# A decoder trunk with its memory values formed token by token, its first output tiles loaded early, and its delta-rule inverses set together by fours

## The chip, the cores and the metric

The kernel runs on one core of a Trainium2 chip. The metric is device time in microseconds of one execution; less is better. The core's engines are TensorE (PE, with its weight loads as PEld), VectorE (DVE), ScalarE (ACT), GpSimd (POOL) and SyncE (SP); all transfers go through the core's 16 DMA engines, issued by SP, by ACT or, in the changed kernel, twice by POOL.

## What is computed

Two layers on a sequence of 1024 tokens of width 1024, with 256 memory tokens for the cross attention. The first layer mixes tokens by an S5 state space model with a gated linear unit (GLU) behind it, the second by a chunked gated delta rule (chunks of 64). Cut to what matters here:

```python
for i in range(2):
    h = rmsnorm(x, norm_w[i]); mem_h = rmsnorm(mem, mem_norm_w[i])
    proj = h @ (s5_w_in if i == 0 else gdn_w_in)
    # layer 0: y = gelu(s5(u) + d*u); y = y * sigmoid(y @ w_glu + b_glu); y_mix = y * silu(gate)
    # layer 1: y_mix = rmsnorm(gated_delta_chunked(...)) * silu(gate)
    k, v = split(mem_h @ w_mem_kv[i]);  y_x = softmax(q k / sqrt(128)) v * silu(gate_x)
    x = x + concat([y_mix, y_x]) @ w_out[i]
return rmsnorm(x, final_norm_w)
# gated delta: per chunk and head  t_mat = (I + strict_lower(k_beta k^T * decay))^-1
```

## The kernel before

Every large product is made of three matmuls of fp32r halves, high by high, low by high and high by low (`mm3`, L48): names that end in h or `hi` are the high half, l or `lo` the low one. A weight tile is loaded as `wraw` (512 KB), its high half `whi` is a cast on ACT (L86), its low half `wlo` a subtraction on DVE (L73), or half of it on DVE and half on POOL. Activations lie feature by token, so that the weights are the stationary operand of 128x512 products.

*Front.* `memory_inputs` loads the memory `memT` (four loads of 256 KB). `memory(0)` weights it by the norm's weight (`mh`, `ml`), and makes eight column tiles of 128 features by 256 tokens with 24 matmuls each: four of keys, four of values. Each tile is multiplied by the row `mrow` of the memory's norms (`kvt`, DVE). A tile of values is then transposed on PE (`ps_a<-ident,kvt`, L51), copied by ACT (`kvu`, L278), and stored. The tokens' x is loaded, weighted (`hh`, `hl`) and projected for two S5 inputs; then `memory(1)` does the second layer's eight tiles. After that, S5 groups and the remaining input tiles of layer 0 run interleaved, with DVE and ACT about as full as PE.

*GLU and output projection.* Twelve GLU tiles (L739 on) read `y`, make 72 matmuls of 512 columns each, and store their result `ye` in DRAM as `yT[ct]`. The attention of layer 0 stores `yT[12]` to `yT[15]` beside it. When all pools of the GLU are closed (`gs.close()`), the loop over two halves of the tokens loads 16 tiles `yr` of `yT` (128x512), splits each to `oh` (ACT) and `ol` (DVE), and projects them to eight column tiles of `w_out`, in the order 12, 13, 14, 15, 0, 1, ..., 11.

*Gated delta units.* `g_units` (L1104 on) writes a table of steps by hand. One step of projection (6 matmuls of 512 columns) stands between two entries. For each of 16 units (chunk, half of the heads) it sets: `prepare` (decays E, from DRAM rows, DVE and the exponentials on ACT, L996), `scores`, `lower` (six transposes `ps_a<-ident,Eb`, which need DVE's `Eb`), `load` (blocks `N`, `T` of a partial inverse, from `Dn`, `Dt` in DRAM), and four stages of `inverse`, each of small products on PE and copies on ACT (`Y1`, L1074; `N`, L1084 to L1098; `Y2`, L1093). PE keeps this order.

*Tail.* `last_column` makes the last output tile in two blocks of 256 tokens, and `out_scale` scales eight tiles by the final norm: most on DVE, those listed in `beside` by ACT and POOL.

Of the kernel before, what the change touches and what calls it, by code (L numbers as in the profile page):

```python
# [22 lines left out]
L = 1024  # L23
# [30 lines left out]
class Kern:  # L54
# [62 lines left out]
    def weight(self, src, cols=128, nk=8):  # L117
        ring = next(self.rings)
        raw = ring.tile([128, nk, cols], F32, name="wraw", tag="wraw")
        hi = ring.tile([128, nk, cols], F32R, name="whi", tag="whi")  # L120
        lo = ring.tile([128, nk, cols], F32R, name="wlo", tag="wlo")
        with self.tc.high_priority(offset=self.ahead):
            self.wq.dma_start(out=raw, in_=src)
            self.split(raw, hi, lo, self.wlo_eng)
        return hi, lo
# [115 lines left out]
    def memory_inputs(self, wp):  # L241
        mt = self.memT = self.once(wp, (128, 8, 256), "memT")
        with self.tc.high_priority(offset=5000):
            self.dma(self.mnw, self.A["mnw"])

            self.act.copy(self.once(wp, (128, 1), "table"), self.ones[:, 0:1])
            for k in range(0, 8, 2):
                self.dma(mt[:, k:k + 2], self.A["memT"][k:k + 2].rearrange("k p t -> p k t"))

    def memory_norm(self, wp):  # L250
# [7 lines left out]
        mcol = self.rstd_cols(wp, acc, 1024, "mn")  # L258
        self.mrow = self.once(wp, (128, 256), "mrow")
        self.rows_to(self.mrow, self.on_partitions(wp, mcol, "mn"))  # L260

    def memory(self, layer, wp):
        mt = self.memT
        hh, hl = self.tl(wp, (128, 8, 256), "mh", F32R), self.tl(wp, (128, 8, 256), "ml", F32R)
        for k in range(8):
            self.weighted(mt[:, k], self.mnw[:, layer, k:k + 1], hh[:, k], hl[:, k])
        if layer == 0:
            self.memory_norm(wp)
        for ct in range(8):
            ps, = self.project([self.A["w_kv"][layer, ct]], (hh, hl), n=256)  # L270
            t = self.tl(wp, (128, 256), "kvt", bufs=2)
            self.tt(t, ps, self.mrow, MUL)
            if ct >= 4:
                pt = self.pa.tile([128, 512], F32, name="ps_a", tag="ps_a")
                for b in range(2):
                    self.pe.transpose(pt[:, 128 * b:128 * b + 128], t[:, 128 * b:128 * b + 128], self.ident)
                t = self.tl(wp, (128, 256), "kvu", bufs=2)
                self.act.copy(t, pt[:, 0:256])  # L278
            self.dma(self.kvd[layer][ct], t)


# [397 lines left out]
    def layer1(self):  # L679
        tc, A = self.tc, self.A  # L680
        P = partial(tc.tile_pool, reuse_waits="tile")
        with P(name="h1", bufs=1) as hp:
            h = self.hidden(hp)
            with P(name="s5p", bufs=1, side="right") as sp:
                with P(name="s5tmp", bufs=1, side="right") as tmp, P(name="mem", bufs=1, side="right") as mp:
                    self.memory_inputs(mp)
                    self.dma(self.nw, A["nw"])
                    self.rings = cycle([self.ring, self.ring, mp])
                    with P(name="ld1", bufs=1, side="right") as wp:
# [6 lines left out]
                        self.wlo_eng, self.wq = "both", self.nc.sync  # L696
                        with self.tc.high_priority(offset=self.ahead):
                            self.memory(0, mp)
                        self.wlo_eng, self.wq = self.v, self.nc.scalar
                        for k in range(KD):  # L700
# [17 lines left out]
                with P(name="s5w", bufs=2, side="right") as wp:  # L718
# [10 lines left out]
                    self.pe.on = False  # L729
            gs = ExitStack()  # L730
            ya = gs.enter_context(P(name="ya", bufs=1, side="right"))
            wp = gs.enter_context(P(name="glu", bufs=2, side="right"))
            ap = gs.enter_context(P(name="at1", bufs=1, side="right"))
            y = []
# [20 lines left out]
        for ct in range(12):  # L755
            w = A["w_glu"][ct]
            ps = self.project([w[:, 0:6], w[:, 6:12]], y)
            e, g = self.tl(wp, (128, L), "ye"), self.tl(wp, (128, L), "ge")
            self.dma(g, self.gate[ct])
            self.tt(e, y[ct][0].bitcast(F32), y[ct][1].bitcast(F32), ADD, self.pool)  # L760
            self.tt(e, e, g, MUL, self.pool)
            for j, p in enumerate(ps):
                s = slice(512 * j, 512 * j + 512)
                sg = self.tl(wp, (128, 512), "sig")
                self.act.activation(sg, p, AF.Sigmoid, bias=self.b_glu[:, ct:ct + 1])
                self.tt(e[:, s], e[:, s], sg, MUL)
            self.dma(self.yT[ct], e)
            for i in range(2):
                next(attend, None)
# [10 lines left out]
        with P(name="yo", bufs=1, side="right") as yp, P(name="x1", bufs=1, side="right") as xp:  # L780
# [3 lines left out]
            for half in range(2):  # L784
                hs, ts_ = slice(512 * half, 512 * half + 512), slice(4 * half, 4 * half + 4)
                y = self.half_tiles(yp, 512, lambda i: 2 if i < 4 else 1)
                for i, k in enumerate([12, 13, 14, 15] + list(range(12))):
                    t = self.tl(xp, (128, 512), "yr", bufs=8)
                    self.dma(t, self.yT[k, :, hs])
                    self.split(t, y[i][0], y[i][1])  # L790
                for ct in range(KD):
# [14 lines left out]
                    else:  # L806
                        sq = self.tl(xp, (128, 512), "sq", bufs=2)
# [3 lines left out]
            self.rows_to(h[2], self.on_partitions(xp, col, "n2"))  # L811
        return st2, h

    def half_tiles(self, yp, n, bufs):
        return [[self.tl(yp, (128, n), f"o{c}{i}", F32R, bufs(i)) for c in "hl"] for i in range(16)]

# [284 lines left out]
    def g_units(self, h, wp, gp):  # L1101
# [32 lines left out]
        for u in range(16):  # L1134
            s = 7 * u
            put(s - 9, prepare, u)
            put(s, scores, u)
            put(s + 5, lower, u)

            s = 80 + 6 * u if u < 4 else 124 + 4 * (u - 4) if u < 10 else 148 + 4 * (u - 10)  # L1140
            put(s - 5, load, u)
            for j in range(4):
                put(s + 3 * j, inverse, u)
        for i, s, n in ((0, 41, 26), (1, 83, 26), (2, 111, 22)):
# [205 lines left out]
    def last_column(self, wp, pieces, y, add, xo, acc):  # L1350
# [229 lines left out]
```

## Time and profile before

| what | value |
|---|---|
| median of 3 runs | 1933.11 us (1930.89 to 1936.47) |
| the profiled execution's own time | 1939.14 us |
| its span on the core | 1937.4 us |
| mean granted TensorE clock | 0.984 |
| PE busy | 1865.1 us, 96% |
| DVE, ACT, POOL busy | 1284.0, 958.1, 95.8 us |
| share of PE in the chain that ended last | 80% |

A row of the windows gives busy time (and instruction counts) of each engine in a stretch, then the clock that TensorE was granted (1.00 is full speed), the share of the DMA engines, and GB/s. A row of the timeline gives the start, the busy time, the engine, line, operation, tiles, and in brackets the idle time just before and what ended it. Times are microseconds from the start of the span.

### The profile page before, as it was taken

To read this page: it belongs to the slowest core of one execution; us is meant where nothing else is said; L and a number is where in the kernel's file an instruction comes from. 1 tells how busy PE (TensorE), PEld (TensorE's weight loads), DVE (VectorE), ACT (ScalarE), POOL (GpSimd) and SP (SyncE) were. 2 spreads that over 40 slices of the span, in tenths; PEclk is the share of its full clock that TensorE was granted. 3 is DMA by queue.
4 is the path that set the end of the run, shared out by engine and by line. 5 is a ranking of instruction groups with operands and counts; after the bars stand their busy time and mean duration, and the time that the engine had idled before them with its cause. 6 is when DMAs were issued, how large, how long until landed. Compare 5 with 4: busy or idle time off the path is not lost.

```text
span 1937.4 us, 28738 instructions
## 1 busy us (share of the span) xinstructions
PE 1865.1 (96%) x10390; PEld 1533.5 (79%) x10390; DVE 1284.0 (66%) x2508; ACT 958.1 (49%) x2043; POOL 95.8 (5%) x65
## 2 busy tenths in 40 slices
PE   6899999999989998999999999999999999899997
PEld 6788888788878887788778878877777888688886
DVE  7988898896565412564455555988743776789744
ACT  5345688786455421543343456665343653544421
POOL 3000000000201221000000000000000000000000
PEclk9999999999999999999999999999999999999999
DMA  7445655655854353654312467676445764876752
GB/s 229 151 136 136 165 170 157 168 155 146 254 167 133 116 173 102 210 164 141 120 56 97 132 199 235 218 224 198 132 117 197 226 202 146 265 231 197 201 161 87
DMA packets 258942, 325.17 MB, mean 168 GB/s; under 512 B 80753, under 2 KB 182705, under 8 KB 258801
## 3 DMA queue, kind: packets, MB, share of 16 engines
q1 hardware_dynamic: 233456, 238.40, 39.9%
q10 hardware_dynamic: 25344, 84.95, 14.7%
q8 instruction: 82, 1.34, 0.3%
q14 instruction: 60, 0.48, 0.1%
HBM read 213.20 MB, written 93.95 MB: 159 GB/s over the span
## 4 chain that ended last, share of the span: by engine, by line
PE 80%; DVE 7%; DMA 6%; ACT 4%; issue 2%; SPq 1%; DVEq 0%; ACTq 0%
PE pp L48 64%; PE ps_a L48 13%; PE ps_a L51 3%; DMA zr<-oTd 1%; SPq L70 1%; DVE wlo L73 1%; DMA yr<-gy 1%; ACT whi L86 0%; DVE pr L77 0%; DMA E<-Grow 0%; DVE ol L73 0%; ACT pr L330 0%; DMA XM<-Dm 0%; DMA R<-E 0%; DMA wraw<-in_s_w_in_dram 0%
## 5 line engine op out<-in xcount | busy, mean ns | idle before, releaser
L48 PE MATMUL pp<-hh,whi 128*128 128x512 f32 x1216 | 496.0, 408 | 0.0
L48 PE MATMUL pp<-hl,whi 128*128 128x512 f32 x1216 | 478.9, 394 | 2.8 <-DVE hl L82 2.8
L48 PE MATMUL pp<-hh,wlo 128*128 128x512 f32 x1216 | 478.0, 393 | 0.0
L86 ACT CAST whi<-wraw 128x1024 fp32r<-128x1024 f32 (+1 forms) x180 | 183.7, 1022 | 370.6 <-PE pp L48 347.0
L73 DVE TENSOR_TENSOR wlo<-wraw,whi 128x1024 fp32r<-128x1024 f32 (+2 forms) x180 | 212.9, 1183 | 94.4 <-ACT whi L86 93.2
L48 PEld LDWEIGHTS pp<-hh,whi 128*128 128x128 f32 x1216 | 229.7, 189 | 50.8 <-issue 5.3
L48 PEld LDWEIGHTS pp<-hh,wlo 128*128 128x128 f32 x1216 | 229.3, 189 | 48.9
L48 PEld LDWEIGHTS pp<-hl,whi 128*128 128x128 f32 x1216 | 230.1, 189 | 46.0 <-DVE hl L82 3.8
L48 PE MATMUL pp<-oh,whi 128*128 128x512 f32 (+1 forms) x528 | 207.8, 394 | 5.7 <-ACT oh L86 5.5
L48 PE MATMUL pp<-oh,wlo 128*128 128x512 f32 (+1 forms) x528 | 210.0, 398 | 0.1
L48 PE MATMUL pp<-ol,whi 128*128 128x512 f32 (+1 forms) x528 | 208.4, 395 | 1.3 <-DVE ol L73 1.3
L48 PEld LDWEIGHTS pp<-oh,whi 128*128 128x128 f32 x528 | 100.9, 191 | 29.0 <-ACT oh L86 7.7
L48 PEld LDWEIGHTS pp<-ol,whi 128*128 128x128 f32 x528 | 100.6, 191 | 25.8 <-DVE ol L73 3.5
L48 PEld LDWEIGHTS pp<-oh,wlo 128*128 128x128 f32 x528 | 101.0, 191 | 21.2 <-DVE wlo L73 0.8
L48 PE MATMUL pp<-yl,whi 128*128 128x512 f32 x288 | 114.2, 396 | 0.4 <-DVE yl L73 0.4
L48 PE MATMUL pp<-yh,wlo 128*128 128x512 f32 x288 | 114.2, 396 | 0.0
L48 PE MATMUL pp<-yh,whi 128*128 128x512 f32 x288 | 113.7, 395 | 0.0
L73 DVE TENSOR_TENSOR pj<-pp,hr 128x512 f32<-128x512 f32 x104 | 69.0, 686 | 54.8 <-PE pp L48 54.8
L73 DVE TENSOR_TENSOR cx<-pp,hr 128x512 f32<-128x512 f32 x48 | 32.5, 689 | 93.6 <-PE pp L48 93.6
L82 DVE SCALAR_TENSOR_TENSOR pj<-cx,conv_w,pj 128x1024 f32<-128x1024 f32 x72 | 92.4, 1283 | 1.4
L48 PEld LDWEIGHTS pp<-yl,whi 128*128 128x128 f32 x288 | 54.4, 189 | 12.4 <-DVE yl L73 0.8
L48 PEld LDWEIGHTS pp<-yh,wlo 128*128 128x128 f32 x288 | 54.4, 189 | 11.9
(363 smaller groups left out, 3109.2 us busy)
## 6 DMA issues: line engine op xcount, KB each, us to landing
wraw<-in_w_out_dram ACTq DMA_DIRECT2D x64, 512.0 KB, 4.1
wraw<-in_g_w_in_dram ACTq DMA_DIRECT2D x44, 512.0 KB, 3.9
wraw<-in_s_w_in_dram ACTq DMA_DIRECT2D x32, 512.0 KB, 4.0
R<-E SPq DMA_DIRECT2D x48, 256.0 KB, 3.9
gate<-pj SPq DMA_DIRECT2D x24, 512.0 KB, 4.4
qkv<-pj SPq DMA_DIRECT2D x24, 512.0 KB, 2.6
kq<-qkv SPq DMA_DIRECT2D x60, 192.0 KB, 4.3
wraw<-in_w_glu_dram ACTq DMA_DIRECT2D x24, 384.0 KB, 3.5
```

The lines of the kernel that those rows point to most:

```text
L48: return self.pin(self.eng.matmul(*a, **kw))
L51: return self.pin(self.eng.transpose(*a, **kw))
L70: self.nc.sync.dma_start(out=out, in_=in_)
L73: (eng or self.v).tensor_tensor(out=out, in0=a, in1=b, op=op)
L82: self.v.scalar_tensor_tensor(out=out, in0=a, scalar=s, in1=b, op0=op0, op1=op1)
L86: self.act.copy(hi, src)
```

## The change

Four places, the diff below cut to its core.

1. *Front.* The two weight tiles of the values of column tiles 4 and 5 are loaded first, in pieces, between the pieces of the memory. Values are made token by feature: the memory's blocks are the stationary operand, and two column tiles of weights are the moving one, so nothing is transposed; ACT scales them by the column `mcol` of the norms into one buffer `kvu`. Values come before keys, and PE is held to the program's order. The sum for the memory's norm is by additions instead of two reductions. `memory(1)` is built in the same way.
2. *GLU to output projection.* `out_inputs` loads and splits `yT[12..15]` and `yT[0]` for the first half of the tokens while the GLU still runs, into tiles of the attention's pool, which stays open. The next ten loads of the first half go straight to tiles of the `yo` pool that are free by then. The last two stores of `yT` are issued by POOL.
3. *Gated delta units.* `lower` comes at step s+7 instead of s+5. The inverses start at steps 84, 88, 92, 96 and then from 120 in fours, with four steps between stages instead of three; the first four have their blocks loaded eight steps ahead.
4. *Tail.* Block 0 of the last scaling has six of its eight tiles on ACT and POOL instead of four.

```diff
+            for q, step in ((0, 2), (1, 4)):
...
+                for k in range(4 * q, 4 * q + 4, step):
+                    raw, hi, lo = (t.rearrange("p (c k) n -> p c k n", c=2)[:, :, k % 4:k % 4 + step] for t in w)
+                    self.dma(raw, self.A["w_kv"][0, 4:6, :, k:k + step].rearrange("c p k n -> p c k n"))
+                    for j in range(k, k + step, 2):
+                        self.dma(mt[:, j:j + 2], self.A["memT"][j:j + 2].rearrange("k p t -> p k t"))
+                    self.split(raw, hi, lo)
...
-            self.v.tensor_reduce(out=part, in_=sq.rearrange("p k t -> p t k"), axis=AX, op=ADD)
+            self.tt(sq[:, 0:2], sq[:, 0:2], sq[:, 2:4], ADD)
+            self.tt(part, sq[:, 0], sq[:, 1], ADD)
...
+                        self.mm3(ps[b].rearrange("p (c n) -> p c n", c=2), (hh[:, k, s], hl[:, k, s]),
+                                 [t[:, j] for t in rows], k == 0, k == 7)
...
-            if ct >= 4:
-                pt = self.pa.tile([128, 512], F32, name="ps_a", tag="ps_a")
-                for b in range(2):
-                    self.pe.transpose(pt[:, 128 * b:128 * b + 128], t[:, 128 * b:128 * b + 128], self.ident)
...
+            t = self.tl(wp, (128, 2, 2, 128), "kvu", bufs=1)
+            for b in range(2):
+                self.act.activation(t[:, :, b], ps[b].rearrange("p (c n) -> p c n", c=2), AF.Copy,
+                                    scale=self.mcol[:, b:b + 1])
...
+            if ct == (0 if layer else 2):
+                for i, ps in enumerate(pairs):
+                    values(i, ps)
...
+            if ct == 10:
+                early = self.out_inputs(ap, wp)
...
-            self.dma(self.yT[ct], e)
+            (self.nc.sync if ct < 10 else self.pool).dma_start(out=self.yT[ct], in_=e)
...
+                    if half == 0 and n < 10:
+                        t = self.tl(yp, (128, 512), f"o{'hl'[n % 2]}{n // 2}")
...
+        for i, y in enumerate(tiles):
+            if i % 2 == 0:
+                raw = self.tl(wp, (128, L), "yr")
+            t = raw[:, 512 * (i % 2):512 * (i % 2) + 512]
+            self.dma(t, self.yT[(12, 13, 14, 15, 0)[i], :, 0:512])
+            self.split(t, *y)
...
-            put(s + 5, lower, u)
+            put(s + 7, lower, u)
...
+            s = 84 + 4 * u if u < 4 else 120 + 4 * (u - 4)
...
-        self.out_scale(wp, xo, rb, 1, blocks[0], (1, 3, 5, 7))
+        self.out_scale(wp, xo, rb, 1, blocks[0], (1, 3, 4, 5, 6, 7))
```

Three places where instructions move, all on ACT, whose products PE waits for. The first is the middle of `memory(0)`. Before, ACT's queue there holds the copies of the transposed values (`kvu`) among the casts of weights (`whi`) and the work on x (`hh`, `sq`):

```order
L86 CAST whi<-wraw 128x1024
L278 COPY kvu<-ps_a 128x256 x2
L179 ACTIVATE sq<-x 128x1024
L237 ACTIVATE hh_167<-x,nw_158 128x1024
L86 CAST whi<-wraw 128x1024
L278 COPY kvu<-ps_a 128x256
L86 CAST whi<-wraw 128x1024
```

Now the values come from the accumulators, and the second pair stands behind two tiles of x:

```order
L86 CAST whi<-wraw 128x1024
L313 ACTIVATE kvu<-ps_a,mcol_381 128x2x128 x2
L86 CAST whi<-wraw 128x1024
L242 ACTIVATE hh_167<-x,nw_158 128x1024
L184 ACTIVATE sq<-x 128x1024
L242 ACTIVATE hh_167<-x,nw_158 128x1024
L184 ACTIVATE sq<-x 128x1024
L313 ACTIVATE kvu<-pp,mcol_381 128x2x128 x2
```

The buffer `kvu` is one now, so the row `kvu<-pp` also waits until the two stores of the row `kvu<-ps_a` have landed; the third key tile on PE takes an accumulator that this row frees.

The second place is the end of the GLU. Before, the casts of the output projection's inputs (`oh`) all follow the last sigmoid (`sig`) and the cast of a small weight (`abw`):

```order
L765 ACTIVATE sig<-pp,b_glu_161 128x512
L86 CAST whi<-wraw 128x1024
L765 ACTIVATE sig<-pp,b_glu_161 128x512
L123 DMA wraw<-in_w_out_dram 128x1024
L86 CAST abw_7023<-abw_7022 128x8x24
L86 CAST oh_7035<-yr 128x512
```

Now five such casts, to tiles of the attention (`qh`, `ph`, `pr`, `q`), stand some forty rows ahead, beside the eleventh GLU tile; these are four of them:

```order
L86 CAST qh<-yr 128x512
L393 CAST ph<-ps_a 128x512 x2
L86 CAST ph<-yr 128x512
L86 CAST whi<-wraw 128x768
L86 CAST ph<-yr 128x512
L128 DMA wraw<-in_w_glu_dram 128x768
L86 CAST pr<-yr 128x512
```

What is left behind the last sigmoid are the casts from the sixth tile on.

The third place is the first group of inverses. Before, one cast of decays (`E`) stands right ahead of two copies of different inverses (`Y`):

```order
L1008 ACTIVATE kq<-ps_a,rk_9686 128x256 x3
L929 ACTIVATE pj<-pj 128x1024
L996 ACT_TABLE_LOAD
L996 ACTIVATE E<-E,gnG_8497 128x128 x6
L1093 COPY Y_11433<-ps_a 64x384
L1074 COPY Y_11448<-ps_a 32x192 x2
L1098 ACTIVATE N_9710<-ps_a 64x6x64
```

Now:

```order
L1171 ACTIVATE N_9675<-ps_a 32x6x32
L1172 ACTIVATE T_132_9679<-ps_a 32x6x32
L1082 ACT_TABLE_LOAD
L1082 ACTIVATE E<-E,gnG_8462 128x128 x6
L1160 COPY Y_11403<-ps_a 32x192 x2
L1184 ACTIVATE N_9674<-ps_a 64x6x64
L1179 COPY Y_11476<-ps_a 64x384
```

The copies of different inverses stand closer together, and a row of decays still stands ahead of them.

More of the change, by code (lines that the diff above doesn't have):

```diff
@@ L246, in memory_inputs, with memory_sum @@
             self.act.copy(self.once(wp, (128, 1), "table"), self.ones[:, 0:1])
-            for k in range(0, 8, 2):
-                self.dma(mt[:, k:k + 2], self.A["memT"][k:k + 2].rearrange("k p t -> p k t"))
-    def memory_norm(self, wp):
+            self.first = []
+            for q, step in ((0, 2), (1, 4)):
+                w = [self.ring.tile([128, 8, 128], dt, name=n, tag=n)
+                     for n, dt in (("wraw", F32), ("whi", F32R), ("wlo", F32R))]
+                self.first.append(w[1:])
+                for k in range(4 * q, 4 * q + 4, step):
[4 more added lines that the diff above has]
+                    self.split(raw, hi, lo)
+    def memory_sum(self, wp):
         acc = self.once(wp, (128, 256), "macc")
@@ L266, in memory @@
             self.weighted(mt[:, k], self.mnw[:, layer, k:k + 1], hh[:, k], hl[:, k])
+        pairs = []
+        for i in range(2):
+            pool, nm = ((self.pa, "ps_a"), (self.pp, "pp"))[i]
+            ps = [pool.tile([128, 256], F32, name=nm, tag=nm) for _ in range(2)]
+            for q in range(2):
+                w = self.first[q] if layer == i == 0 else self.value_weight(layer, i, q)
+                rows = [t.rearrange("p (c k) n -> p k c n", c=2) for t in w]
+                for j in range(4):
+                    k = 4 * q + j
+                    for b in range(2):
+                        s = slice(128 * b, 128 * b + 128)
+                        self.mm3(ps[b].rearrange("p (c n) -> p c n", c=2), (hh[:, k, s], hl[:, k, s]),
+                                 [t[:, j] for t in rows], k == 0, k == 7)
+            pairs.append(ps)
@@ new lines, in values @@
+        def values(i, ps):
+            t = self.tl(wp, (128, 2, 2, 128), "kvu", bufs=1)
+            for b in range(2):
+                self.act.activation(t[:, :, b], ps[b].rearrange("p (c n) -> p c n", c=2), AF.Copy,
+                                    scale=self.mcol[:, b:b + 1])
+            for c in range(2):
+                self.dma(self.kvd[layer][4 + 2 * i + c], t[:, c].rearrange("p b d -> p (b d)"))
+        todo = []
+        for ct in range(4):
+            if ct == (0 if layer else 2):
+                for i, ps in enumerate(pairs):
+                    values(i, ps)
+            ps, = self.project([self.A["w_kv"][layer, ct]], (hh, hl), n=256)
+            todo.append((ct, ps))
+            if layer == 0 and ct == 2:
+                self.mrow = self.once(wp, (128, 256), "mrow")
+                self.rows_to(self.mrow, self.on_partitions(wp, self.mcol, "mn"))
+            if layer or ct >= 2:
+                for one in todo:
+                    key(*one)
+                todo = []
@@ L811, in layer1, with out_inputs, half_tiles @@
             self.rows_to(h[2], self.on_partitions(xp, col, "n2"))
+        as1.close()
         return st2, h
-    def half_tiles(self, yp, n, bufs):
-        return [[self.tl(yp, (128, n), f"o{c}{i}", F32R, bufs(i)) for c in "hl"] for i in range(16)]
+    def out_inputs(self, ap, wp):
+        two = [self.tl(ap, (128, 2, 512), nm, F32R) for nm in ("ph", "pl")]
+        tiles = [[self.tl(ap, (128, 512), nm, F32R) for nm in ("qh", "ql")]]
+        tiles += [[t[:, b] for t in two] for b in range(2)]
+        tiles.append([self.tl(ap, (128, 512), nm, F32R) for nm in ("q", "sg")])
+        pr = self.tl(ap, (128, 2, 512), "pr", F32R)
+        tiles.append([pr[:, i] for i in range(2)])
+        for i, y in enumerate(tiles):
[4 more added lines that the diff above has]
+            self.split(t, *y)
+        return tiles
+    def half_tiles(self, yp, n, bufs, down=False):
+        order = range(15, -1, -1) if down else range(16)
+        y = {i: [self.tl(yp, (128, n), f"o{c}{i}", F32R, bufs(i)) for c in "hl"] for i in order}
+        return [y[i] for i in range(16)]
     def s5_input(self, i, h, wp):
```

48 lines of the change are left out of this document (30 added, 18 removed).

## Prediction

> **What bounds the kernel now.** I read the page's busy shares first (PE 96%), then the windows by stage, the waits of PE, and the timeline of PE at the longest of these. Of the windows, these stretches matter:
>
> ```profile
> 105.00:340.00 235.00, 235.00 (x1302) 195.06 (x1301) 200.79 (x382) 157.15 (x315) 0.00 (x0) 1.00 0.55 153
> 760.00:785.00 25.00, 19.29 (x66) 14.22 (x65) 13.23 (x20) 11.77 (x20) 0.00 (x0) 0.80 0.52 161
> 1140.00:1160.00 20.00, 16.54 (x70) 13.48 (x70) 10.77 (x14) 15.58 (x34) 0.00 (x0) 0.91 0.75 246
> 1285.00:1320.00 35.00, 30.53 (x276) 24.45 (x275) 29.86 (x59) 20.55 (x48) 0.00 (x0) 0.95 0.75 220
> ```
>
> PE is full where nothing is said of it, as from 105 to 340. So what can be won is idle time of PE, and with it stretches where the granted clock falls (0.80, 0.91, 0.95 here). The waits of PE name the places that this change touches:
>
> ```profile
> PE pp L48 <- ACT oh L86: 5.5, 2, 3.6
> PE ps_a L51 <- DVE kvt L73: 5.2, 2, 2.8
> PE ps_a L51 <- DVE Eb L73: 4.1, 3, 3.5
> PE ps_a L48 <- DVE fndg L79: 4.0, 1, 4.0
> PE ps_a L48 <- ACT Y L1093: 3.1, 1, 3.1
> PE pp L48 <- DVE hl L82: 2.8, 2, 2.0
> ```
>
> An idle stretch costs more than itself. At the start of the output projection (timeline of PE):
>
> ```profile
> 766.73 0.39 PE L48 MATMUL pp<-yh,wlo 128*128 128x512 f32 x1
> 770.74 0.50 PE L48 MATMUL pp<-oh,whi 128*128 128x512 f32 x1 [3.63 <-ACT oh L86]
> ...
> 775.83 0.80 PE L48 MATMUL pp<-oh,whi 128*128 128x512 f32 x1 [1.86 <-ACT oh L86]
> ...
> 780.14 0.63 PE L48 MATMUL pp<-oh,whi 128*128 128x512 f32 x1
> 780.56 0.63 PE L48 MATMUL pp<-ol,whi 128*128 128x512 f32 x1
> ...
> 781.40 0.39 PE L48 MATMUL pp<-oh,whi 128*128 128x512 f32 x1
> 781.63 0.39 PE L48 MATMUL pp<-ol,whi 128*128 128x512 f32 x1
> ```
>
> From start to start a matmul of 512 columns takes 0.42 us at 780 and 0.23 at 781.4: after the idle time PE ran at half speed. The Trainium skill ("TensorE: Matmul & The Clock Gate", Part 1: The HAM clock gate) has the same two rates and a window of about 3.4 us after which full speed returns; the trace agrees with the rates, and here the slow stretch lasts about 10 us, because a second idle time falls into it.
>
> **The change part by part.**
>
> *Output projection.* 18 matmuls of 512 columns stand between 766.73 + 0.23 and 781.40, that is 14.4 us for 18 x 0.23 = 4.1 us of work: 10.3 us are lost, 5.7 of them idle. Now 5 of 16 inputs lie ready; their 15 matmuls (15 x 0.23 = 3.4 us) run at once. Their loads and casts lie beside the last two GLU tiles, where ACT has room (11.77 of 25 us busy in the window above, most of it behind the GLU). The sixth input's cast still comes behind the last sigmoid, about when the idle time now ends (3.6 us behind the GLU), so those 3.4 us cover it or nearly, and the casts behind it, half of 1.05 us each, keep ahead of three matmuls (0.69). What is late next is the last input, `yT[11]`: POOL issues its store, and its load and cast must follow. No row shows a transfer from POOL. The page's lines for SP and ACT (section 6) bound it:
>
> ```profile
> gate<-pj SPq DMA_DIRECT2D x24, 512.0 KB, 4.4
> qkv<-pj SPq DMA_DIRECT2D x24, 512.0 KB, 2.6
> ```
>
> With an estimated 3 us for the last sigmoid and product of `ye`, 2.6 to 4.4 for the store, 4 for the load and 1.3 for cast and split, `yT[11]` is ready 11 to 13 us behind the GLU. By the order of PE its first matmul is the 51st behind the GLU, 50 x 0.23 = 11.4 us. I take a wait of 1.5 us: gain 8.5 us, with 4 (POOL's store 5 us late, and a slow clock behind it) and 10 as ends. The Trainium skill ("DMA: Bandwidth & Descriptors", Anatomy of one DMA) gives about 2.0 us plus bytes by 436 GB/s for a transfer issued by POOL, 3.2 us for this store by its fit; no run here shows it, and the sum by it would be the same.
>
> *Front.* These rows carry it (PE's timeline, the last three being the first matmul on x, of `memory(1)`, and behind it; and the first uses on ACT):
>
> ```profile
> 10.98 0.58 PE L48 MATMUL pp<-mh,whi 128*128 128x256 f32 x1 [10.98 <-ACT whi L86]
> 39.52 0.44 PE L51 MATMUL ps_a<-ident,kvt 128*128 128x128 f32 x2 [2.81 <-DVE kvt L73]
> 47.22 0.39 PE L48 MATMUL pp<-hh,whi 128*128 128x512 f32 x1
> 77.09 0.28 PE L48 MATMUL pp<-mh,whi 128*128 128x256 f32 x1
> 77.21 0.28 PE L48 MATMUL pp<-ml,whi 128*128 128x256 f32 x1
> 104.71 0.39 PE L48 MATMUL pp<-hh,whi 128*128 128x512 f32 x1
> 4.91 1.71 ACT L237 ACTIVATE mh<-memT,mnw 128x256 fp32r<-128x256 f32 x4 [2.62 <-DMA memT<-in_memT_dram]
> ```
>
> A matmul of 256 columns takes 0.12 us (77.09 to 77.21), so 192 of them take 23 us, once per layer, before and after alike. The first memory piece is on hand at 4.91 us; the first weight piece (256 KB, half the cast of 1.05 us) goes just ahead of it, so PE can start at about 6.2 instead of 10.98: 4.8 us. The eight transposes of layer 0 go (8 x 0.11 = 0.9), and the wait of 2.81 with a slow stretch behind it (1.7: half of one 3.4 us stretch, as at 1150 below). The waits on `hl` (2.8) go if the x loads come no later. Against this stands a new wait: the third key tile needs the accumulators of the second pair of values, and the row that frees them stands on ACT behind two tiles of x, about 1.15 + 1.05 us each, and behind the landing of two stores. The values' scale is known by about 25 us, the stores are issued by 28 and land near 31.5, and the row ends near 33.5, when PE wants it at 28 to 29: 5 us, and up to 3 us of slow clock. I take 6.5. Sum to 77.09: 4.8 + 0.9 + 2.8 + 1.7 + 2.8 - 6.5 = 6.5 us. In `memory(1)` the other `kvt` wait (5.2 - 2.81 = 2.4), a slow stretch (1.7) and eight transposes (0.9) go; the stores of its values have all of the second pair's time to land: 5 us. DVE loses two reductions and eight of 16 `kvt` products, and ACT eight copies, so neither is later. Together 11.5 us at 104.7.
>
> Does that pass through the S5 stage, where DVE is busy 201 of 235 us? The waits of DVE in that stretch:
>
> ```profile
> DVE pj L73 <- PE pp L48: 12.7, 5, 5.6
> DVE vs L73 <- ACT vw L642: 8.0, 6, 3.3
> DVE wbt L73 <- DMA bcs<-in_s_bc_dram: 5.1, 1, 5.1
> ```
>
> DVE waits for PE for 12.7 us in all, so PE leads there and DVE has about as much slack as PE wins. I take 2 us as lost on the way: 9.5 us for the front, with ends of 2 (all slack already used, and the new wait at 10) and 14.
>
> The half-speed start is in the sum as it was. By the same section of the Trainium skill, about 3.4 us of steady work would end it; before, it lasted from 10.98 until about 23.6 with two idle stretches in it, so the sum by that rule would be up to 4 us lower if the pieces come in time. That no row shows.
>
> *Gated delta units.* These rows, of PE and ACT:
>
> ```profile
> 1150.27 1.54 PE L51 MATMUL ps_a<-ident,Eb 128*128 128x128 f32 x6 [3.46 <-DVE Eb L73]
> 1311.94 1.05 PE L48 MATMUL ps_a<-Y,T 64*64 64x64 f32 x13 [3.06 <-ACT Y L1093]
> 1309.67 1.86 ACT L996 ACTIVATE E<-E,gnG 128x128 f32<-128x128 f32 x6
> 1311.44 0.45 ACT L1093 COPY Y<-ps_a 64x384 f32<-64x384 f32 x1
> ```
>
> `lower` two steps later puts 12 matmuls (2.7 us) into the wait of 3.46; the rest of `Eb` waits (0.6) goes, and with 0.7 us of idle time left there is no slow stretch (the clock of 0.91 over 20 us is 1.7 us): 5 us. For the inverses, the wait of 3.06 and its slow stretch (0.95 over 35 us, 1.7) come from a copy queued behind decays that were late. The order shows such a row of decays still ahead of the copies, but a stage now has four steps (5.5 us) instead of three. On the other side the first four start four steps apart instead of six, so that more copies stand behind each of the decays of steps 82, 89 and 96; and the other twelve start at 120 instead of 124, with their loads three steps (4 us) earlier, while their blocks are made in the same steps as before: a load that has to wait for them is a new wait of PE. I take a gain of 1 us, between +5 (the wait goes) and -5 (one more like it): 6 us for the stage, ends 0 and 10.
>
> *Tail.* On DVE the last norm's chain holds two scalings fewer:
>
> ```profile
> 1926.29 0.16 DVE L77 TENSOR_SCALAR fzh<-fzv 128x2 f32<-128x2 f32 x1
> 1926.35 0.47 DVE L82 SCALAR_TENSOR_TENSOR xo<-xo,fnw,ps_a 128x256 f32<-128x256 f32 x1
> 1926.74 0.31 DVE L79 TENSOR_SCALAR fze<-fze 128x2 int32<-128x2 int32 x1
> ```
>
> Each takes 0.4 us of a chain that PE waits 4.0 us for: 0.8 us. POOL has six products instead of four and is done before the last block needs it. Ends 0 and 1.2.
>
> **The sum.** 8.5 + 9.5 + 6 + 0.8 = 24.8 us off the profiled execution's 1939.14, to 1914.3. That execution lies 6 us above the median of 1933.11; off the median it is 1908.3, and I say 1909.
>
> **The rivals.** *The front's gain is used up in the S5 stage or by the new `kvu` wait.* For it: DVE is at 85% of that stage, and PE has waits on DVE and ACT behind it already. Against it: the 12.7 us above. Without the front's 9.5 us the time is 1918. *The last input comes late.* The stores by POOL are the one price that no row shows; with 5 us more and a slow stretch of the kind at 771 to 781, 7 us of the 8.5 are gone: 1916. *The change does less than it says*: the early inputs' loads wait for the last stores of `yT` or for space, and the front's pieces come as late as now. Then 5 us of the units and the tail are left: 1927. *Slower:* the store of `yT[11]` by POOL is slow in itself, since its price is the one that no row bounds from above. The first column can't end without it, and PE runs out of other work once it has the second column's ready inputs too: at 40 us instead of 4.4 the time is 1909 + 36 = 1945, and from 28 us on the change loses. Against it: POOL is idle there (0.00 in the window 760 to 785), and nothing else of POOL stands behind the store.
>
> **How the numbers follow.** The forecast, within its own ends, has 0.62; the front lost 0.12; the late input 0.1; less than it says 0.07; slower by POOL's store 0.05; 0.04 for gains beyond the upper ends. The ends added give 2 + 4 + 0 + 0 = 6 us off, 1927, and 14 + 10 + 10 + 1.2 = 35 us off, 1898. The range, 1897 to 1926, holds nearly all of that, with the lost front and the late input, and leaves out the slower case and most of "less than it says". A measurement of this kernel can tell about 0.3% from no change, 5.8 us. Faster by more are all cases but the slower one and half of "less than it says" (1927 is on the border): 0.9, rounded; within 0.3%: 0.05; slower: 0.05.
>
> **What would show it.** Right: PE starts near 6 us, its first matmul on x near 42, `memory(1)` near 70, `pp<-hh` behind it near 93; the window behind the GLU has a clock near 1.00 and under 3 us of idle time; the `Eb` waits sum to about 1 us; the chain's `fndg` wait is 3.2. Wrong: a wait of PE on `kvu` above 8 us; waits on DVE in 105 to 340 that are not there now; `oh` or `ol` waits above 4 us; waits on `Y` or `N` more than twice in the units' second group.

## The result, and the profile after

| what | before | after |
|---|---|---|
| median | 1932.0 us (4 runs, 1930.22 to 1936.47) | 1909.73 us (4 runs, 1907.34 to 1911.74) |
| the profiled execution's own time | 1939.14 us | 1910.86 us |
| its span | 1937.4 us | 1909.0 us |
| mean granted clock | 0.984 | 0.985 |

The ratio is 0.9884 (95% interval 0.9868 to 0.99): faster by 22.3 us, where the prediction said 24.1 for the median (24.8 for the profiled execution). The total came out near the forecast; its terms did not. PE's timeline cuts the span into stages, each from one instruction of PE to another. The last three columns are the kernels that have one part alone, told further down.

| stage on PE | before | after | e1 front | e2 output | e3 units |
|---|---|---|---|---|---|
| start to the last `ps_a<-S,wc` (S5 done) | 495.1 | 488.2 | 484.9 | 493.4 | 491.0 |
| to the last GLU matmul | 271.6 | 271.4 | 267.8 | 270.8 | 269.7 |
| to the last of the output projection | 189.4 | 183.9 | 188.8 | 181.4 | 188.7 |
| to the first `gt,tri` of layer 1 | 27.3 | 25.6 | 27.3 | 25.1 | 25.0 |
| to the first `ident,vT` (units done) | 508.0 | 495.0 | 508.5 | 506.1 | 491.6 |
| to the end | 446.0 | 445.0 | 445.2 | 447.0 | 445.5 |

In this table, stages that a kernel does not touch differ by up to 4 us between runs, which is the least uncertainty of any one cell. The units' stage can differ by more: with the same code for the units as in the changed kernel it took 492.0 to 501.7 us in the later runs.

**The waits.** Of PE's waits after, those that bear on the change, in us together, times, longest:

```profile
PE pp L48 <- ACT kvu L313: 6.0, 1, 6.0
PE ps_a L48 <- DVE fndg L79: 4.8, 1, 4.8
PE pp L48 <- DVE wlo L73: 2.2, 1, 2.2
PE pp L48 <- ACT oh L86: 2.1, 3, 1.4
PE ps_a L48 <- DMA N<-Dn: 1.4, 2, 0.9
PE pp L48 <- DVE hl L82: 1.1, 1, 1.1
```

`Eb` (4.1 before) is gone and `oh` fell from 5.5 to 2.1; `kvu` is the new wait that was forecast at 5; `fndg`, the scale of the last norm that PE needs for the last block, is longer than before, not shorter.

**The front.** PE's timeline after, at the first matmul, a wait for weights, the wait for `kvu`, the first matmul on x, the start of `memory(1)` and what follows it:

```profile
5.36 0.58 PE L48 MATMUL ps_a<-whi,mh 128*128 128x256 f32 x1 [5.36 <-ACT mh L242]
...
17.23 0.36 PE L48 MATMUL pp<-wlo,mh 128*128 128x256 f32 x1 [2.17 <-DVE wlo L73]
...
36.71 0.58 PE L48 MATMUL pp<-mh,whi 128*128 128x256 f32 x1 [5.96 <-ACT kvu L313]
...
46.73 0.50 PE L48 MATMUL pp<-hh,whi 128*128 128x512 f32 x1 [1.00 <-DVE kvt L73]
...
78.25 0.28 PE L48 MATMUL ps_a<-whi,mh 128*128 128x256 f32 x1
...
101.04 0.39 PE L48 MATMUL pp<-hh,whi 128*128 128x512 f32 x1
```

PE starts 5.6 us earlier than before and comes to x only 0.5 us earlier. The windows say where the rest went: before, then after, from 24 us to x and from x to `memory(1)`:

```profile
24.00:47.20 23.20, 20.39 (x159) 20.19 (x158) 16.84 (x18) 12.84 (x15) 8.67 (x5) 0.93 0.78 242
47.20:77.00 29.80, 26.99 (x132) 21.45 (x131) 27.41 (x65) 12.77 (x19) 4.59 (x2) 1.00 0.36 120
```

```profile
24.00:47.00 23.00, 16.04 (x110) 15.62 (x109) 21.20 (x31) 15.71 (x19) 7.52 (x4) 0.85 0.83 278
47.00:78.00 31.00, 29.37 (x127) 23.97 (x127) 25.65 (x76) 7.90 (x14) 2.87 (x1) 0.89 0.26 82
```

Up to x, PE works 4.4 us less than before in the same time, at a lower clock: the 7.0 us in which it stands are the wait for `kvu` and the one for `kvt`, the scaled keys. From x on it waits less than before (1.6 us idle instead of 2.8) and is still 1.6 us slower, since the clock is 0.89, not 1.00: 31 x 0.11 = 3.4 us. In the clock's record the half-speed stretches of the front are 18.6 to 22.0, 35.7 to 42.5 and 59.6 to 66.4; before they were 40.7 to 44.1 and 95.3 to 98.7. The half-speed start stands ahead of these: full speed is on record from 8.4 us on, 3.0 us behind PE's first matmul, and before from 23.6 us on, 12.6 us behind it. Up to there a matmul of 256 columns takes 0.21 us from start to start, then 0.12.

The wait itself is as predicted. ACT after, around it:

```profile
29.54 0.83 ACT L313 ACTIVATE kvu<-ps_a,mcol 128x256 f32<-128x256 f32 x2
...
31.63 1.14 ACT L242 ACTIVATE hh<-x,nw 128x1024 fp32r<-128x1024 f32 x1
...
36.19 0.84 ACT L313 ACTIVATE kvu<-pp,mcol 128x256 f32<-128x256 f32 x2 [0.48 <-DMA kv<-kvu]
```

The second pair of values stands behind two tiles of x and then, for its last 0.48 us, behind the stores of the first pair, since there is one buffer. These stores land at about 36.1 us, where 31.5 was forecast, so by this row it would have been as late without the two tiles.

**Behind the GLU.** Four stretches of the windows after (front of S5, end of the GLU, first `Eb`, first group of inverses):

```profile
95.00:330.00 235.00, 235.00 (x1322) 196.19 (x1321) 202.41 (x383) 152.92 (x308) 0.00 (x0) 1.00 0.55 155
745.00:775.00 30.00, 28.01 (x113) 21.42 (x112) 13.10 (x19) 10.79 (x17) 1.82 (x3) 0.97 0.66 216
1115.00:1135.00 20.00, 19.34 (x84) 15.14 (x83) 11.31 (x30) 8.71 (x19) 4.67 (x9) 1.00 0.70 233
1260.00:1300.00 40.00, 36.06 (x366) 29.04 (x365) 35.00 (x64) 24.30 (x56) 0.00 (x0) 0.91 0.75 217
```

The second and third are nearly full now (2.0 and 0.7 us idle), at a clock of 0.97 and 1.00 instead of 0.80 and 0.91. The fourth is no better than before, 3.9 us idle in 40 and a clock of 0.91 (4.5 in 35 and 0.95); yet the units' stage is 13 us shorter. What is left behind the GLU is one wait for `oh` above 1 us, and SP's queue tells why. Timeline of SP's loads of the output projection's inputs, and of PE:

```profile
753.33 0.42 SPq L70 DMA_DIRECT2D oh<-yT  x1
759.81 0.32 SPq L70 DMA_DIRECT2D ol<-yT  x1
760.17 0.43 SPq L70 DMA_DIRECT2D oh<-yT  x1
767.33 0.32 SPq L70 DMA_DIRECT2D ol<-yT  x1
```

```profile
771.35 0.50 PE L48 MATMUL pp<-oh,whi 128*128 128x512 f32 x1 [1.41 <-ACT oh L86]
```

The ten loads should be issued in a row; SP stands still twice, for 6.1 and 6.7 us. ACT issued loads of weights (`wraw<-in_w_out_dram`) at 753.88 and 762.21, whose landing takes 5.5 us (median of this stretch); the trace puts SP's 12.8 us of waiting here down to these two loads. That SP's next load waits for the completion semaphore that each of them had used last is argued from the program's dependencies.

**The units.** One round of four stages of inverses with the four steps of projection between them. Timeline of PE before, the first of its four groups (the others start at 1444.54, 1446.97 and 1449.39, and the round ends with the row at 1451.16):

```profile
1442.14 0.39 PE L48 MATMUL pp<-hh,wlo 128*128 128x512 f32 x1
1442.46 0.57 PE L48 MATMUL ps_a<-N,L 32*32 32x32 f32 x24
1442.95 0.50 PE L48 MATMUL pp<-hh,whi 128*128 128x512 f32 x1
1443.29 0.40 PE L48 MATMUL pp<-hl,whi 128*128 128x512 f32 x1
...
1451.16 0.39 PE L48 MATMUL pp<-hh,wlo 128*128 128x512 f32 x1
```

And after, where the four groups of a round are one:

```profile
1403.36 0.39 PE L48 MATMUL pp<-hh,wlo 128*128 128x512 f32 x1
1403.68 0.73 PE L48 MATMUL ps_a<-Y,T 64*64 64x64 f32 x9
...
1405.44 0.54 PE L48 MATMUL ps_a<-N,L 32*32 32x32 f32 x22
1405.91 0.50 PE L48 MATMUL pp<-hh,whi 128*128 128x512 f32 x1
...
1411.27 0.39 PE L48 MATMUL pp<-hh,wlo 128*128 128x512 f32 x1
```

Starts are four steps apart and stages too, so stage 0 of one unit, 1 of the one before, 2 and 3 of those ahead fall on the same step. Both rounds hold the same 84 small matmuls and 24 large ones. Before it takes 1451.16 - 1442.14 = 9.02 us, after 1411.27 - 1403.36 = 7.91: 1.1 us less per round, with no idle time in either and at full speed. Between a large matmul and the first small one lie 0.32 us instead of 0.23, and behind the first large one after a group 0.34 (1443.29 - 1442.95); before, a round pays this four times, now once. The Trainium skill ("TensorEngine Tiling (Array Packing)", Key Properties) says that a change of the tiling mode drains TensorE; the rows agree that it costs, and put a price on it, which the page does not.

The same can be read over the whole stage. Windows of the units' stage before, after, in e4 (stages three steps apart again, told below) and in e9 (the slowest run of this stage with the changed table):

```profile
983.43:1491.39 507.96, 497.86 (x3374) 401.03 (x3374) 321.74 (x506) 247.85 (x626) 6.59 (x11) 0.99 0.54 166
969.03:1464.03 495.00, 487.82 (x3374) 401.84 (x3374) 321.02 (x506) 247.23 (x626) 6.59 (x11) 0.99 0.55 170
963.09:1469.21 506.12, 498.64 (x3374) 400.05 (x3374) 322.09 (x506) 246.21 (x626) 6.59 (x11) 0.99 0.54 167
964.67:1466.33 501.66, 489.61 (x3374) 403.37 (x3374) 321.54 (x506) 246.55 (x626) 6.57 (x11) 0.98 0.54 168
```

PE does the same 3374 matmuls in each. Take from its busy time what the half-speed stretches on record add (3.4, 6.8, 3.4 and 8.5 us): 494.4, 481.0, 495.2 and 481.1 us are left. Over all runs it is 494.2 to 495.2 us in the four kernels with three steps between stages and 480.4 to 481.1 in the nine with four. So the new table saves PE 13.4 us of work, whatever the waits and the clock of a run are; in e9 the stage is longer by waits (12.0 us idle instead of 7.2, 5.8 of it for `N<-Dn`) and slow clock alone.

**The tail.** DVE's timeline after, in the chain of the last norm (`fzv`, `fze`, `fzh` and `fzt`, which end in `fndg`), and POOL's beside it:

```profile
1896.61 0.50 DVE L77 TENSOR_SCALAR fze<-fzv 128x2 int32<-128x2 int32 x1
...
1897.14 0.65 DVE L79 TENSOR_SCALAR fze<-fze 128x2 int32<-128x2 int32 x1
1897.82 1.32 DVE L82 SCALAR_TENSOR_TENSOR fzt<-fze,fzh 128x1 f32<-128x1 f32 x2
...
1899.37 0.35 DVE L82 SCALAR_TENSOR_TENSOR fzt<-fze,fzh 128x1 f32<-128x1 f32 x2
```

```profile
1894.99 4.14 POOL L73 TENSOR_TENSOR xo<-xo,fr 128x256 f32<-128x256 f32 x6 [61.89 <-ACT fr L1466]
```

The pair `fzt` takes 1.32 us while POOL works (until 1899.13) and 0.35 when it has ended; 4.14 / 6 = 0.69 us is one product of POOL, and 0.65 or 0.66 is what each of the slow instructions takes.

### The profile page after: what moved, and what is told of

It is laid out like the page before. It is cut to its first block, busy times and chain, and to the rows that moved or that the text cites. A ratio compares the mean times of both kernels' runs of the same rounds, so it can differ in the third digit from the quotient of the medians.

```text
span 1909.0 us, 28670 instructions
## 1 busy us (share of the span) xinstructions
PE 1846.5 (97%) x10374; PEld 1528.0 (80%) x10374; DVE 1284.1 (67%) x2501; ACT 957.8 (50%) x2046; POOL 98.4 (5%) x67
## 3 DMA queue, kind: packets, MB, share of 16 engines
q10 hardware_dynamic: 25344, 84.95, 14.7%
## 4 chain that ended last, share of the span: by engine, by line
PE 81%; DVE 6%; DMA 6%; ACT 3%; issue 2%; SPq 1%; POOL 0%; ACTq 0%; DVEq 0%; POOLq 0%
PE pp L48 65%; PE ps_a L48 13%; PE ps_a L51 3%; DVE wlo L73 1%; SPq L70 1%; DMA zr<-oTd 1%; DMA yr<-gy 1%; DMA N<-Dn 1%; ACT whi L86 0%; ACT pr L382 0%; DVE XN L73 0%; DVE XT L73 0%; DMA vT<-qkv 0%; DVE acc L73 0%; DMA q<-qx 0%
## 5 line engine op out<-in xcount | busy, mean ns | idle before, releaser
L86 ACT CAST whi<-wraw 128x1024 fp32r<-128x1024 f32 (+2 forms) x181 | 183.5, 1015 | 340.5 <-PE pp L48 305.7
L48 PE MATMUL pp<-oh,whi 128*128 128x512 f32 (+1 forms) x488 | 191.6, 393 | 2.2 <-ACT oh L86 2.1
L48 PE MATMUL pp<-ol,whi 128*128 128x512 f32 (+1 forms) x488 | 191.3, 393 | 0.9 <-DVE ol L73 0.9
L48 PE MATMUL pp<-oh,wlo 128*128 128x512 f32 (+1 forms) x488 | 191.8, 394 | 0.0
L48 PEld LDWEIGHTS pp<-oh,whi 128*128 128x128 f32 x488 | 92.5, 190 | 23.6 <-ACT oh L86 3.7
L48 PEld LDWEIGHTS pp<-ol,whi 128*128 128x128 f32 x488 | 92.5, 190 | 22.3 <-DVE ol L73 2.6
L48 PEld LDWEIGHTS pp<-oh,wlo 128*128 128x128 f32 x488 | 92.4, 189 | 19.1 <-DVE wlo L73 0.3
L48 PEld LDWEIGHTS pp<-yl,whi 128*128 128x128 f32 x288 | 54.2, 188 | 12.6 <-DVE yl L73 1.1
L48 PEld LDWEIGHTS pp<-yh,whi 128*128 128x128 f32 x288 | 54.3, 189 | 12.0 <-ACT yh L86 0.4
```

The lines of the kernel that those rows point to most:

```text
L48: return self.pin(self.eng.matmul(*a, **kw))
L86: self.act.copy(hi, src)
```

## The experiments

Eleven kernels, in three groups, each group on one chip with the kernel before beside it.

**e1 to e3: each part alone.** The kernel before with part 1, 2 or 3 of the change; the key line of each is

```diff
+    ps = [pool.tile([128, 256], F32, name=nm, tag=nm) for _ in range(2)]   # e1: the whole of part 1
+                early = self.out_inputs(ap, wp)                            # e2: the whole of part 2
+                put(s + 4 * j, inverse, u)                                 # e3: the whole of part 3
```

> The kernel before with the change's front alone. If the lead seen at the end of the GLU (7 us) is the front's own, the time is 7 us under the kernel before (ratio 0.9963). If part of that lead is another part's (pool order in the GLU) or chance in the S5 stage, it is 2 to 4 us under it. Its first matmul on x should come near 46.8 us as in the changed kernel, with one wait of 6 us on kvu.

> The kernel before with the GLU and output projection's part alone. Theory: 7 us under the kernel before (5.6 in the stage and 1.7 from one slow clock window fewer behind it). Rival: the slow window behind it is a matter of where the windows fall, and 5 to 6 us are left. PE's waits on oh should be about 2 us instead of 5.5.

> The kernel before with the gated delta units' table alone. Theory (stages of different units fall on one step and run as one batch on PE): 12 to 13 us under the kernel before, 5 of them from the Eb wait. Rival (only waits go): 5 from Eb and 1 to 4 from the inverses, 6 to 9 us.

Measured: e1 1923.17 us, ratio 0.9958 (0.9943 to 0.9973), by the ratio 8.1 us; e2 1925.4, 0.997 (0.9955 to 0.9985), 5.8 us; e3 1915.27, 0.9924 (0.99 to 0.9947), 14.7 us. In e1 the interval, some 5 to 11 us, holds the 7 us of the front's own and leaves out the 2 to 4; e2 can't tell its 7 us from the 5 to 6 of its rival; in e3 the interval, some 10 to 19 us, holds the 12 to 13 of the theory and leaves out the 6 to 9 of the rival. The three gains add up to 28.6 us with some 6 us of uncertainty, more than the 22.3 of the joined change with its 3; the difference is about as large as the two uncertainties together. The units are the largest part, not the smallest but one.

**e4: stages three steps apart again.** All of the change, but

```diff
-                put(s + 4 * j, inverse, u)
+                put(s + 3 * j, inverse, u)
```

> The changed kernel with three steps between the stages of an inverse instead of four, starts and loads as changed, so that the stages of different units fall on different steps. Batch theory: a batch of 84 small matmuls holds PE for 2.32 us, and the four apart for 0.59 + 0.93 + 0.94 + 0.60 = 3.06, so this loses 0.74 us for each of about 11 batches, 8 us against the changed kernel (1918). Rival (waits of the inverse matter): within 3 us of the changed kernel (1907 to 1913).

Measured: 1917.01 us, ratio 0.9926 (0.9903 to 0.9949). By the ratios this is 8 us behind the changed kernel, with some 5 of uncertainty, as the batch theory said. The units' stage takes 506.1 us instead of 495.0, and by the windows above PE's work in it is back at 495.2. On PE there are 64 groups of small matmuls in the inverses' stretch, where the changed kernel has 22 and the kernel before 58. PE's waits in the stretch hardly differ: 5.5 us of idle time inside groups in both kernels. So it is the number of groups that counts, not the time that a copy has: 36 groups fewer than before at 0.37 us each (a third of the 1.1 us of a round) are 13.3 us, and 13.4 were found.

**e5: the second pair of values into another buffer.** The buffer of the squares is free by then; with it, the row comes ahead of the two tiles of x on ACT:

```diff
-            t = self.tl(wp, (128, 2, 2, 128), "kvu", bufs=1)
+            if i:
+                t = self.tl(wp, (128, 4, 256), "msq").rearrange("p a (b c) -> p (a b) c", b=2)[:, 0:4].rearrange("p (a b) c -> p a b c", a=2)
+            else:
+                t = self.tl(wp, (128, 2, 2, 128), "kvu", bufs=1)
```

> The changed kernel with the second pair of values scaled into the free space of the tile msq instead of into kvu again, so that this no longer waits for the stores of the first pair to land; ACT's order puts it ahead of the two tiles of x. If the wait of 6.0 us of the third key tile is that row's place and its wait for the stores, PE resumes about 4 us earlier and the slow clock windows from 35.8 to 42.6 shrink: 4 to 7 us under the changed kernel at the first matmul on x. Rival: x's own chain (ACT hh, DVE hl, DMA) is as late, and its waits take the place: 0 to 2 us.

Measured: 1906.48 us, ratio 0.9871 (0.9852 to 0.9891). PE's timeline in e5, at the third key tile and at x:

```profile
30.95 0.39 PE L48 MATMUL pp<-mh,whi 128*128 128x256 f32 x1 [2.27 <-ACT msq L316]
...
39.17 0.50 PE L48 MATMUL pp<-hh,whi 128*128 128x512 f32 x1 [1.77 <-DVE kvt L73]
```

The wait falls from 5.96 to 2.27 us, half-speed clock between the start and 47 us is on record for 3.4 us (40.2 to 43.6) instead of 10.2, and x comes 7.6 us earlier than in the changed kernel. Of that lead 4.9 us are left behind `memory(1)` and 3.1 behind the S5 stage: waits for `hl` (1.03 and 1.25 us), for the norm of layer 0 (`n1dg`, 1.20) and, in the S5 stage, for `wbt` (1.12, with a half-speed stretch) take its place. At x the theory holds, with a little more than its 4 to 7 us; behind it, waits of the kind that the rival named use more than half of this up. The median moves by less than the runs scatter.

**e6 and e11: SP's standstill.** In e6 the two weight loads of the first half's second column are issued by POOL instead of ACT; in e11 besides, the last two stores of `yT` by SP again:

```diff
+                    self.wq = self.pool if half == 0 and ct == 1 else self.nc.scalar   # e6, e11
...
-            (self.nc.sync if ct < 10 else self.pool).dma_start(out=self.yT[ct], in_=e)
+            self.dma(self.yT[ct], e)                                                   # e11
```

> The changed kernel with the two weight loads of the output projection's second column (first half) issued by POOL instead of ACT. Theory: loads on SP of yT[6] and yT[8] stand still at 753.5 and 760.3 because each DMA takes one of a few completion semaphores in turn and must wait until the one that had it before, a weight load of ACT, has landed; with those on POOL's queue SP goes through, the wait on oh (1.4 us) and its slow window (1.7) go: 3 us less. Rival: SP stands still for the tiles or for yT itself, and nothing changes (within 1 us).

> As e6 (ACT's weight loads of the first half's second column moved to POOL's queue, so that SP's loads do not stand still), but the stores of yT[10] and yT[11] are issued by SP again, ahead of those loads. Theory (in e6 the last input waited for POOL's store, 4 to 5 us to landing, behind which its load comes): SP's stores land about 2 us after issue by the page's row of stores before, the wait on oh falls from 2.2 us in e6 to under 1 us and the stretch from the end of the GLU to the end of the first output projection is 1 to 2 us shorter than in e6. Rival (the loads on SP queue behind the stores, or the last input is late by its own sigmoid and product): the wait stays at 1.4 to 2.2 us.

Measured: e6 1908.22 us, ratio 0.9884 (0.9862 to 0.9905); e11 1911.88, 0.9896 (0.987 to 0.9922). SP's timeline in e6, the first and the last of ten loads, and the cast of the last input on ACT:

```profile
746.49 0.32 SPq L70 DMA_DIRECT2D oh<-yT  x1
...
752.38 0.38 SPq L70 DMA_DIRECT2D ol<-yT  x1
```

```profile
768.38 0.62 ACT L86 CAST oh<-yr 128x512 fp32r<-128x512 f32 x1 [4.44 <-DMA yr<-yT]
```

The standstill is gone: all ten loads are issued within 6 us. So SP did stand behind ACT's loads. But it was hiding another wait: the last input, `yT[11]`, is stored by POOL at 758.28 and loaded from 763.41 on, and PE waits 2.2 us for it at the longest. e8, which has the same edit, shows no standstill and a wait of 2.1 us; the seven kernels that have the change's second part and the standstill wait 0.2 to 1.4 us at the longest in this stretch. So to take the standstill away gains nothing. In e11, SP and PE:

```profile
758.30 0.32 SPq L70 DMA_DIRECT2D yT<-ye  x1
758.72 0.38 SPq L70 DMA_DIRECT2D oh<-yT  x1
```

```profile
765.53 0.80 PE L48 MATMUL pp<-oh,whi 128*128 128x512 f32 x1 [6.63 <-ACT oh L86]
```

The theory loses; the rival's reason holds, at three times its price. All ten loads stand on SP's queue behind the last store, which waits for its product until 758.3; PE waits 6.6 us, and the stage is 189.2 us long, as before the change (189.4; e6 184.0). Nor does SP's store land in the 2 us of the theory, or sooner than POOL's: 5.6 us here (median of the two; 5.4 and 5.1 in the kernel before), against 4.9 by POOL in the changed kernel. Without the two stores on POOL, one line of the diff, this stage gains nothing: they keep SP's queue free for the loads. In the medians e6 and e11 can't be told from the changed kernel.

**e7 and e10: the tail.** In e7 the list of tiles beside DVE is the old one; in e10 POOL's six products of the first block are left out:

```diff
-        self.out_scale(wp, xo, rb, 1, blocks[0], (1, 3, 4, 5, 6, 7))
+        self.out_scale(wp, xo, rb, 1, blocks[0], (1, 3, 5, 7))     # e7
...
+                if len(beside) < 6:                                # e10
                     self.tt(xo[k][:, s], xo[k][:, s], r, MUL, self.pool)
```

> The changed kernel with the tail as before (four tiles on ACT and POOL instead of six). Theory: while POOL runs its products, DVE's short operations of the last norm's chain take 0.65 us instead of 0.16; with POOL done 1.4 us earlier the wait for fndg is 4.05 instead of 4.77 us, though two more scalings stand in the chain: 0.7 us less, which shows in the trace and not in the time. Rival: the longer wait was chance of that run, and it is 4.8 to 5.6 here.

> The changed kernel with the six products of POOL in the first block of the last scaling left out; DVE's instructions and ACT's are the same. Theory (POOL's products slow DVE's short instructions of the last norm): the two fzt instructions of the first step take 0.35 us as in the later steps instead of 1.32, fze 0.3 instead of 0.65, and the wait on fndg falls from 4.77 to 3.2 to 3.6 us, the gain that was forecast. Rival (the chain waits for something else, for instance the transfers of the scaled tiles that are issued at the same time): the durations and the 4.77 us stay.

Measured: e7 1908.01 us, ratio 0.987 (0.985 to 0.9891), with a wait of 4.05 us on `fndg`, as in the kernel before, against 4.77. In e10 (one run, 1901.15 us; its output lacks the products) it is 2.98, and DVE's chain reads:

```profile
1888.79 0.16 DVE L77 TENSOR_SCALAR fze<-fzv 128x2 int32<-128x2 int32 x1
1888.86 0.16 DVE L77 TENSOR_SCALAR fzh<-fzv 128x2 f32<-128x2 f32 x1
1888.98 0.17 DVE L79 TENSOR_SCALAR fze<-fze 128x2 int32<-128x2 int32 x1
1889.19 0.35 DVE L82 SCALAR_TENSOR_TENSOR fzt<-fze,fzh 128x1 f32<-128x1 f32 x2
```

Every slow instruction is at its short time, with the same instructions on DVE and ACT. This settles it: POOL's products slow DVE's short ones, and the change put two more of them beside the chain. The Trainium skill has the rule that the prediction did not weigh: "SBUF — State Buffer" (SBUF: two separate sides) says that the two engines share one pair of ports as an exclusive lock, held for a whole instruction, against DVE instructions with two inputs there or in a mode that reads by both ports. The rows agree in size: each slow instruction is held for up to one product of POOL. Why `fze`, which has one input, is held and `fzh` beside it (0.15 us) is not, no run here shows.

**e8 and e9: the best of these together.** e8 has the edits of e5, e6 and e7, e9 those of e5 and e7.

> The three edits of this call together. If they add: 4 + 3 + 0.7, 6 to 10 us under the changed kernel, about 1902. If the S5 stage or x's chain takes up what the front wins: 3 us under it.

> The changed kernel with two edits: the second pair of values goes into the free buffer of the memory's squares (as in e5), and the last scaling has its four tiles beside DVE again (as in e7). Theory: the tail edit takes 0.7 us from the wait on fndg (4.77 to 4.05) and the buffer takes 3.3 us off the end of the S5 stage (as measured in e5), the two don't meet: 4 us below the changed kernel, 1905 to 1906 on a chip where the kernel before takes 1931. Rival: what the front wins is used up behind the S5 stage, and only the tail's 0.7 us is left: 1909.

Measured: e8 1903.69 us, ratio 0.9865 (0.9844 to 0.9886); e9 1906.95, 0.9869 (0.9843 to 0.9894). Each has its waits as its parts do (`fndg` 4.1 and 4.0, the second pair of values 2.4), and the lowest ratios of all; from the changed kernel's 0.9884 neither can be told apart. By the ratios e8 is 3.7 us and e9 2.9 us under it with some 5 us of uncertainty, so neither run settles whether the parts add.

## Why the prediction was right, and where it was not

On the profiled execution it gave 24.8 us, and 28.4 were found; on the median 24.1 (1933.11 to 1909) and 22.3. That the total fits is in part luck: the units won 7 us more than forecast, the other three parts 5.3 us less. By parts, in us of the profiled execution:

| part | forecast | found |
|---|---|---|
| front, at the end of the S5 stage | 9.5 | 7.0 |
| GLU to layer 1 | 8.5 | 7.2 |
| units | 6 | 13.0 |
| tail, by the wait on `fndg` | +0.8 | -0.7 |

The stages that were not to change gave the rest, about 2. Of its signs of being right, the first matmul on x near 42, `memory(1)` near 70, the matmul behind it near 93 and the `fndg` wait of 3.2 did not come.

*Front.* The start (5.4 instead of 6.2), the wait on `kvu` (5.96 instead of 5, with stores that landed 4.6 us later than forecast) and `memory(1)` (27.6 to 22.8 us, a gain of 4.8 against 5.0) are right. The step that failed is the sum to 77.09: 6.5 us were to be won and 1.2 were lost. An earlier start ran into inputs that were not there: waits of 0.71 (`mh`), 0.59 and 2.17 us (`wlo`), where the start of before had one of 1.11 and one of 0.84. And slow clock was priced too low: a stretch of 6.8 us at half speed lies on the wait of 6 us, of which PE worked 5.8 and lost 2.9, one of 3.4 us (1.7 lost) behind the one on `wlo`, and one of 6.8 (3.4 lost) behind x. The waits on `hl` were to go "if the x loads come no later"; one of 1.14 us stayed.

All this was hidden in part by a gain that the sum left out. It took the half-speed start "as it was", and this start cost 5.3 us before (12.6 us, 2.0 of them idle) and 1.5 after: 3.8 us won, the "up to 4 us" that the prediction named beside its sum. It is no firm property of the new front: with the front of before, full speed comes at 15.3 us in e2 and 16.0 in e3, with the new one at 8.4 to 11.0 in nine kernels and at 17.8 in e8, where PE stood still for 1.0 us in between. What sets it, no run here settles. So the profiled run of the kernel before was slow in its front: x came at 47.2 us there, at 45.6 and 42.7 in e2 and e3, and at 45.7 to 46.8 in the seven kernels with the new front and its one buffer `kvu`. Up to x the new front wins nothing that these runs can tell. The first matmul behind `memory(1)` comes at 97.5 to 101.0 us instead of 101.0 to 104.7, and the end of the S5 stage, where the lead is firm, at 484.9 to 488.2 instead of 491.0 to 495.1.

The other step that failed is that 2 us are lost in the S5 stage: 3.3 were won there (390.4 us to 387.1). All three kernels without the new front (before, e2, e3) have a half-speed stretch of 6.8 us in that stage, at 351 to 361, worth 3.4 us; the changed kernel, e1, e6, e10 and e11 have none there, the other five one of 3.4 us. So the rival in which the S5 stage uses the gain up falls for the change itself, though e5 shows that the way to its end takes more than half of anything further.

*GLU to layer 1.* The early inputs do what was said. The forecast put the last wait, 1.5 us, on `yT[11]` by POOL's store; it is 1.41 us, but in this run the late inputs are those that SP issued behind ACT's loads, which no row before could show and the forecast did not consider. With that taken away (e6) the store's input is as late, so the term was right in size on two grounds at once. That is luck: the wait came out as forecast by a cause that the forecast did not have.

*Units.* The `Eb` term is exact, 5.0 us: the lead over the kernel before grows from 14.4 to 19.4 us across that wait. The step that failed is "for the inverses ... a gain of 1 us": it weighed only waits. These did stay about as they were, as was said: one of 3.1 us on `Y` and one of 1.1 on `N` went, waits on `N<-Dn` of 1.4 and of 3.5 without a named releaser came, and the half-speed stretches in the inverses rose from one to four. What it missed is the 1.1 us that each merged round saves; ten rounds have all four groups in one, 11 us, and with those that merge in part 13.4 us of PE's work go, which come back in e4. Against that stand the three stretches more of slow clock, 5.1 us. The order could have shown it: with equal distances of starts and stages the four rows of different units stand together.

*Tail.* "0.8 us" had the sign wrong. The two scalings did leave DVE's chain; POOL's products, taken as free, cost more than they saved (e7, e10).

## What to carry to other kernels

Count the places where PE changes between large and small tiles, not only its waits: letting the small products of several units fall on the same step saved 13.4 us here, about as much as all waits of that stage with their slow clock cost before (10.1 and 3.4 us). A transfer that must wait for its data belongs on a queue on which nothing useful stands behind it. An earlier start is worth only what the next late input leaves of it, and each idle stretch of a microsecond or two should be priced with the slow clock behind it.

## What the hardware showed that was not expected

- Small products: a change from 128x512 matmuls to tiles of 32 or 64 and back costs about 0.2 us (0.09 in front of the group and 0.11 behind its first large matmul), and a group has a part of its own that does not shrink with it: from large matmul to large matmul, 84 small ones take 2.32 us in one group (1403.36 to 1405.91, less 0.23) and 3.05 in four. Together a group less saves 0.37 us.
- POOL's product of 128x256 (0.69 us) holds up DVE instructions on two columns, from 0.17 to 0.65 us each; one on `fzh` beside them kept its 0.15.
- A store of 512 KB issued by POOL took 4.9 us to land and one by SP in the same place 5.6. By the fit that the prediction cites from the Trainium skill ("DMA: Bandwidth & Descriptors", Anatomy of one DMA), an estimated 3.2 us, POOL's is 1.7 us later in this stretch, in which the loads of weights and inputs run too.
- Loads on one queue can stand behind loads of another: SP for 6.1 and 6.7 us behind two weight loads of ACT, and no longer when those were moved (e6).
